# ScalarE's passes over the decay rows of a chunk, queued behind the rounding of the chunk in front

## The chip, the core and the metric

The kernel runs on one core of a Trainium2 chip. The metric is the time of one execution in microseconds (us) on the device. The engines are TensorE (PE in the profile, its weight loads PEld), VectorE (DVE), ScalarE (ACT), GpSimd (POOL) and SyncE (SP), which issues nearly all DMAs. Each engine runs its instructions in the order in which they stand in its own queue, and waits for other engines and for DMAs by semaphores.

## The reference, cut to what matters

One layer of a streaming encoder trunk on 2048 tokens of width 1024, in float32: RMSNorm, an input projection, two token mixers that read it (a short gated convolution and a Mamba-2 scan), an output projection, a second RMSNorm and a squared-ReLU MLP, and a last RMSNorm. The part that the change touches is the scan, here as the reference has it:

```
seg = a_cum[:, :, :, None] - a_cum[:, :, None, :]
decay = jnp.exp(jnp.where(causal[None, None, :, :, None, None], seg, -jnp.inf))
scores = jnp.einsum("bclgn,bcsgn->bclsg", c_c, b_c)
y_diag = jnp.einsum("bclsgr,bcsgrp->bclgrp", scores[..., None] * decay, x_c)
decay_end = jnp.exp(a_cum[:, :, -1:] - a_cum)
states = jnp.einsum("bclgn,bclgrp->bcgrpn", b_c, x_c * decay_end[..., None])
```

For each chunk of tokens and each head there is a matrix of decays, the exponential of a difference of running sums. It multiplies the scores, and the product multiplies the tokens' x (the diagonal part, y_diag). Beside that, x weighted by the decay up to the chunk's end is multiplied by B and added to a state that goes on to the next chunk.

## The kernel before, in words

The tokens lie in four blocks of 512 columns. Large products are float32 products made of three matmuls each: a rounded value (hi) and its remainder (lo) on both sides, hi by hi, hi by lo and lo by hi (`mm3`, L112 to L115, and L281 to L283 in `chain`). Rounding to hi is a ScalarE copy, the remainder a VectorE subtraction. The input projection and the MLP run seven half-size products in place of eight for each pair of tiles.

The program goes through these stages: the first half of the projection (to about 460 us), the second half with the first half of the scan beside it (to about 960 us), the output projection with the second half of the scan beside it (to about 1250 us), then the MLP up and down and the last norm. The scan is a generator: the loops of the stage take one piece of it after each product, so that its small instructions stand between the large matmuls. The order that each engine gets is then set by a scheduler, which takes the instructions by their place in the program, as they become ready in its own account of time; it may put an instruction of a later chunk ahead of one of an earlier chunk if that one isn't ready. `tc.issue_after(ins)` adds an edge to it: what is recorded inside stands behind `ins` on the engine of `ins`.

The scan has 32 steps (`CHUNKS`, L1212), numbered 0 to 31 here: for each block of 512 tokens, two groups of eight heads, four chunks of 128 tokens each. Steps 0 to 15 run beside the projection with one buffer of each kind, steps 16 to 31 beside the output projection with two (`bufs`, L1222). A step has these parts:

- `load` (L1238): DMAs of B and C (tile `bc`), of x (`xd`) and of the running sums of eight heads, broadcast to all partitions (`dec`, L1255, from `rd_d`).
- `front`, first piece (L1284 to L1296): TensorE transposes x and B (`ptx`, `ptb`) and multiplies B by C; ScalarE copies x to `xtok` (L1291) and rounds B (`btok`, L1293).
- `front`, second piece (L1299 to L1308): VectorE multiplies `xtok` by two weights (L1301). ScalarE rounds the product for the state (L1303, `xtok<-stmp`, the "rounding of weighted x"); VectorE makes its remainder (L1308). ScalarE goes over the decay rows: eight passes, one for each head (L1306, Relu with the head's bias), and one exponential over all (L1307).
- `front`, third piece: ScalarE scales x by D (L1311), VectorE multiplies the decays by the masked scores (L1312).
- `back` (L1315): TensorE multiplies B by the rounded x (`st`, L113 to L115), C by the state (`yo`, L1326) and the decays by x (`yd`, L1329). VectorE combines them (L1338 to L1345), ScalarE squares (L1348) and takes a root (L1356) for a norm, and a DMA stores the result.

The passes over the decay rows need only a DMA, while the rounding needs TensorE, ScalarE and VectorE in turn. With two buffers the rows of step n+1 are on the chip while step n is under way, and so the scheduler places passes of step n+1 ahead of the rounding of step n. Beside the scan, ScalarE also rounds the weights of the output projection (L100, `whi`) and the blocks of mixer output that it multiplies (L1458 scales `ry` after a DMA, L1459 rounds it).

Of the kernel before, what the change touches and what calls it, by code (L numbers as in the profile page):

```python
# [2 lines left out]

# [1 line left out]

# [8 lines left out]
AF = mybir.ActivationFunctionType  # L14
# [11 lines left out]
HG = 8  # L26
# [14 lines left out]
def trunk(ctx: ExitStack, tc: tile.TileContext, x, w_in, w_dt, w_out, w_up, w_down, cvec, hrow, out):  # L41
    nc = tc.nc
# [42 lines left out]
    def col(base, i):  # L85
        return cv[:, base + i : base + i + 1]
# [37 lines left out]
    def psum(tag, name, bufs=1):  # L124
        if tag in turns:
            tag = next(turns[tag])
        return ps.tile([P, 512], F32, tag=tag, name=name, bufs=bufs)

    class Rstd:


        def __init__(self, pool, tmp, n, w):
            self.pool, self.tmp, self.scale, self.w, self.n = pool, tmp, 1.0 / n, w, w // P
# [1078 lines left out]
    CHUNKS = [(b, g, c) for b in range(NB) for g in range(G) for c in range(NC)]  # L1212

    class Scan:
        def __init__(self, pool):
            self.state = []
            for g in range(G):
                s0 = pool.tile([P, 512], F32, name=f"state{g}")
                nc.vector.memset(s0, 0.0)
                self.state.append(s0)  # L1220
# [57 lines left out]
        def front(self, n):  # L1278

            b, g, c, h, ts, r0 = self.place(n)  # L1280
            t = self.got[n]
            bT, cT = t["bc"][:, 0], t["bc"][:, 1]
            byhead = lambda a: a.rearrange("p (h d) -> p h d", h=HG)
            pt = psum("tp", "ptx", 2)  # L1284
            for j in range(4):
                nc.tensor.transpose(pt[:, j * P : (j + 1) * P], t["xd"][:, j], ident)
            pb = psum("tp", "ptb", 2)
            nc.tensor.transpose(pb[:, 0:P], bT, ident)
            nc.tensor.matmul(pb[:, P : 2 * P], bT, cT, start=True, stop=True)
            xtok = self.tile([512], "xtok", 1)  # L1290
            nc.scalar.copy(xtok, pt)  # L1291
            hi, lo = t["btok"] = self.tile([P], "btok", 1).bitcast(F32R), bT.bitcast(F32R)
            nc.scalar.copy(hi, pb[:, 0:P])  # L1293
            nc.vector.tensor_tensor(out=lo, in0=pb[:, 0:P], in1=hi.bitcast(F32), op=ALU.subtract)
            sm = self.tile([L], "smask", 1)
            nc.vector.tensor_tensor(out=sm, in0=pb[:, P : 2 * P], in1=tri, op=ALU.mult)  # L1296
            yield

            for k, by in (("xde", "dend"), ("xdt", "dt")):  # L1299
                t[k] = self.tmp()  # L1300
                nc.vector.tensor_tensor(out=byhead(t[k]), in0=byhead(xtok), in1=t[by], op=ALU.mult)  # L1301
            hi, lo = t["parts"] = [a.bitcast(F32R) for a in (self.tile([512], "xtok", 1), self.tmp())]
            nc.scalar.copy(hi, t["xde"])  # L1303
            dec = t["dec"]
            for i in range(HG):
                nc.scalar.activation(dec[:, i], dec[:, i], AF.Relu, bias=t["a"][:, i : i + 1], scale=-1.0)  # L1306
            nc.scalar.activation(dec, dec, AF.Exp, scale=-1.0)  # L1307
            nc.vector.tensor_tensor(out=lo, in0=t["xde"], in1=hi.bitcast(F32), op=ALU.subtract)  # L1308
            yield
            for j in range(4):  # L1310
                nc.scalar.mul(t["xd"][:, j], t["xd"][:, j], col(C_D, 4 * g + j))  # L1311
            nc.vector.tensor_tensor(out=dec, in0=dec, in1=sm.unsqueeze(1).to_broadcast([P, HG, L]), op=ALU.mult)  # L1312
            yield
# [49 lines left out]
        def run(self, begin, end):  # L1363
# [10 lines left out]
            if self.bufs == 1:  # L1374
                for n in range(begin, end):
                    back = self.back(n)
                    front = self.front(n + 1) if n + 1 < end else iter(())
                    next(back)
                    yield
                    next(back)  # L1380
                    self.load(n + 1)
                    self.load_rows(n + 1)
                    yield
                    next(back)
                    yield
                    yield
                    next(front, None)
                    yield
                    next(back)
                    yield  # L1390
                    next(front, None)
                    yield
                    next(back)
                    self.load_gate(n + 1)
                    yield
                    next(front, None)
                    yield
                return
# [281 lines left out]
```

## Time and profile before

| | |
|---|---|
| median of 3 runs | 2637.45 us (2635.89 to 2637.7) |
| the profiled execution's own time | 2629.58 us |
| its span, first to last instruction | 2627.8 us |
| busy: PE, PEld, DVE, ACT | 99%, 81%, 73%, 55% of the span |
| mean granted TensorE clock | 0.998 |
| DMA, read from and written to HBM | 354.89 MB, 179.83 MB |

A group's line in the profile names the line of the kernel, the engine, the operation, the tiles (written <- read) and shapes, the count, the busy time with the mean duration, and the time that the engine sat idle just before, with what ended it. A line of the timeline begins with its start and its duration in us, and has such an idle time in brackets at its end. A matmul of 512 columns is shown for 0.39 us, but in an undisturbed row the next one starts 0.23 us later: they overlap, so a wait of TensorE is read from the starts. Matmuls in plain float32 show as two records each.

### The profile page before, as it was taken

How to read it: one execution, taken by the hardware profiler on the slowest of the kernel's cores; microseconds unless marked ns; L12 is line 12 of the kernel's file. 1: busy time of each engine (PE TensorE's matmuls, PEld its weight loads, DVE VectorE, ACT ScalarE, POOL GpSimd, SP SyncE). 2: the span in 40 equal slices, each digit the busy share in tenths (PEclk: the TensorE clock that was granted, in tenths of full speed). 3: DMA queues.
4: the chain of work that ended last, by engine and by line, in shares of the span. 5: the costliest groups of instructions: out<-in, count | busy, mean ns of one | idle time of the engine just before them, and what ended most of it. 6: DMA issues, size and time to landing. Idle time of an engine off the chain costs nothing.

```text
span 2627.8 us, 33775 instructions
## 1 busy us (share of the span) xinstructions
PE 2602.0 (99%) x12136; PEld 2140.6 (81%) x12136; DVE 1918.4 (73%) x2634; ACT 1455.3 (55%) x2211; POOL 55.7 (2%) x98
## 2 busy tenths in 40 slices
PE   9999999999999999999999999999999999999998
PEld 7888888788888888888888888888887788888887
DVE  7978867777778777878777765644448777888985
ACT  6654345776667676867336555655555444444443
POOL 0010000000000000000000000000000000000001
PEclk9999999999999999999999999999999999999999
DMA  3545745555555588877666786855558544665762
GB/s 147 203 171 192 273 144 194 190 167 172 176 167 164 165 281 255 267 225 223 201 201 235 271 311 229 285 205 206 186 200 288 154 152 151 208 213 170 247 208 77
DMA packets 252167, 536.96 MB, mean 204 GB/s; under 512 B 26208, under 2 KB 93024, under 8 KB 252000
## 3 DMA queue, kind: packets, MB, share of 16 engines
q1 hardware_dynamic: 251856, 534.29, 60.8%
q8 instruction: 95, 1.56, 0.2%
q14 instruction: 72, 0.59, 0.1%
q10 hardware_dynamic: 144, 0.52, 0.1%
HBM read 354.89 MB, written 179.83 MB: 203 GB/s over the span
## 4 chain that ended last, share of the span: by engine, by line
PE 65%; issue 24%; DMA 4%; ACT 3%; DVE 3%; SPq 0%; POOL 0%; POOLq 0%; DVEq 0%; ACTq 0%
PE px L281 10%; PE px L283 10%; PE px L282 10%; PE py L281 5%; PE py L282 5%; PE py L283 5%; PE pm L114 4%; PE pm L113 4%; PE pm L115 3%; PE pw L281 2%; PE pw L283 2%; PE pw L282 2%; DMA dec<-rd_d 1%; PE yd L1329 1%; PE yo L1326 1%
## 5 line engine op out<-in xcount | busy, mean ns | idle before, releaser
L281 PE MATMUL px<-uh,whi 128*128 128x512 f32 x1672 | 656.4, 393 | 9.6 <-DVE acc L1051 6.4
L282 PE MATMUL px<-ul,whi 128*128 128x512 f32 x1672 | 651.7, 390 | 0.0
L283 PE MATMUL px<-uh,wlo 128*128 128x512 f32 x1672 | 651.6, 390 | 0.0
L281 PEld LDWEIGHTS px<-uh,whi 128*128 128x128 f32 x1672 | 314.1, 188 | 83.7 <-DVE acc L1051 6.0
L101 DVE TENSOR_TENSOR wlo<-wraw,whi 128x1024 fp32r<-128x1024 f32 x214 | 222.6, 1040 | 202.6 <-ACT whi L100 202.5
L283 PEld LDWEIGHTS px<-uh,wlo 128*128 128x128 f32 x1672 | 314.3, 188 | 66.0 <-issue 0.2
L282 PEld LDWEIGHTS px<-ul,whi 128*128 128x128 f32 x1672 | 314.2, 188 | 63.7
L100 ACT CAST whi<-wraw 128x1024 fp32r<-128x1024 f32 x214 | 193.9, 906 | 309.3 <-PE px L282 219.2
L100 ACT CAST whi<-s 128x1024 fp32r<-128x1024 f32 x210 | 219.8, 1047 | 224.0 <-PE py L282 95.9
L281 PE MATMUL py<-uh,whi 128*128 128x512 f32 x836 | 327.1, 391 | 1.1 <-ACT eb L784 0.8
L282 PE MATMUL py<-ul,whi 128*128 128x512 f32 x836 | 325.8, 390 | 0.0
L283 PE MATMUL py<-uh,wlo 128*128 128x512 f32 x836 | 325.5, 390 | 0.0
L101 DVE TENSOR_TENSOR wlo<-s,whi 128x1024 fp32r<-128x1024 f32 x210 | 255.3, 1216 | 70.2 <-ACT whi L100 68.5
L113 PE MATMUL pm<-uh,whi 128*128 128x512 f32 (+1 forms) x648 | 250.9, 388 | 0.1
L114 PE MATMUL pm<-ul,whi 128*128 128x512 f32 (+1 forms) x648 | 248.2, 383 | 0.4 <-DVE ul L211 0.2
L115 PE MATMUL pm<-uh,wlo 128*128 128x512 f32 (+1 forms) x648 | 247.9, 383 | 0.0
L281 PEld LDWEIGHTS py<-uh,whi 128*128 128x128 f32 x836 | 157.1, 188 | 35.6 <-ACT eb L784 1.2
L283 PEld LDWEIGHTS py<-uh,wlo 128*128 128x128 f32 x836 | 156.9, 188 | 32.7
L282 PEld LDWEIGHTS py<-ul,whi 128*128 128x128 f32 x836 | 157.0, 188 | 32.3
L352 ACT CAST uh<-rh 128x1024 fp32r<-128x1024 f32 (+1 forms) x128 | 120.2, 943 | 85.3 <-PE py L283 67.2
L281 PE MATMUL pw<-uh,whi 128*128 128x512 f32 x418 | 163.3, 391 | 0.0
L283 PE MATMUL pw<-uh,wlo 128*128 128x512 f32 x418 | 162.7, 389 | 0.0
(242 smaller groups left out, 3788.4 us busy)
## 6 DMA issues: line engine op xcount, KB each, us to landing
hid_d<-e SPq DMA_DIRECT2D x96, 512.0 KB, 3.7
rh<-hid_d SPq DMA_DIRECT2D x96, 512.0 KB, 4.4
wraw<-w_in SPq DMA_DIRECT2D x68, 512.0 KB, 4.0
wraw<-w_down SPq DMA_DIRECT2D x104, 256.0 KB, 3.6
wraw<-w_up SPq DMA_DIRECT2D x48, 512.0 KB, 4.2
dec<-rd_d SPq DMA_DIRECT2D x32, 512.0 KB, 5.1
wraw<-w_out SPq DMA_DIRECT2D x32, 512.0 KB, 4.7
x_d<-xt SPq DMA_DIRECT2D x64, 256.0 KB, 3.8
```

The source lines that it names most:

```text
L100: nc.scalar.copy(hi, raw)
L101: eng.tensor_tensor(out=lo, in0=raw, in1=hi.bitcast(F32), op=ALU.subtract)
L113: nc.tensor.matmul(out, whi, hi, start=(k == 0), stop=False)
L114: nc.tensor.matmul(out, whi, lo, start=False, stop=False)
L115: nc.tensor.matmul(out, wlo, hi, start=False, stop=(k == nk - 1))
L281: nc.tensor.matmul(p, hi, h[0], start=not seeded and k == 0, stop=False, **kw)
L282: nc.tensor.matmul(p, hi, h[1], start=False, stop=False, **kw)
L283: nc.tensor.matmul(p, lo, h[0], start=False, stop=(k == len(g) - 1), **kw)
L352: nc.scalar.copy(p[i][0], t)
L1326: nc.tensor.matmul(yo[:, j * L : (j + 1) * L], state[:, j * P : (j + 1) * P], cT, start=True, stop=True)
L1329: nc.tensor.matmul(yd[(i % 2) * 64 : (i % 2) * 64 + 64, (i // 2) * L : (i // 2 + 1) * L], byhead(t["xdt"])[:, i, :], t["dec"][:, i % 2 * 4 ...
```

## The change

In `front`, the eight passes over the decay rows are recorded ahead of the rounding, and inside `tc.issue_after` of the rounding of the step before. No instruction is added, taken away or given another size.

```
     class Scan:
+        cast = None
+
...
             hi, lo = t["parts"] = [a.bitcast(F32R) for a in (self.tile([512], "xtok", 1), self.tmp())]
-            nc.scalar.copy(hi, t["xde"])
             dec = t["dec"]
-            for i in range(HG):
-                nc.scalar.activation(dec[:, i], dec[:, i], AF.Relu, bias=t["a"][:, i : i + 1], scale=-1.0)
+            with tc.issue_after(self.cast.ins) if self.cast else nullcontext():
+                for i in range(HG):
+                    nc.scalar.activation(dec[:, i], dec[:, i], AF.Relu, bias=t["a"][:, i : i + 1], scale=-1.0)
+            self.cast = nc.scalar.copy(hi, t["xde"])
             nc.scalar.activation(dec, dec, AF.Exp, scale=-1.0)
             nc.vector.tensor_tensor(out=lo, in0=t["xde"], in1=hi.bitcast(F32), op=ALU.subtract)
```

In the changed kernel the lines stand two or three further down: the passes are L1308, the rounding L1309, the exponential L1310, and the copy to `xtok` L1293, the copy for `btok` L1295, the scaling by D L1314, the square L1351, `ry` L1461 and L1462. In the following pieces of ScalarE's queue the numbers behind the tiles tell buffers apart: `dec_9565` belongs to step 24, `xtok_9651` to step 23, `dec_10669` to step 30, `xtok_10759` to step 29, `dec_9376` to step 23 and `xtok_9452` to step 22.

ScalarE around the rounding of step 23, before:

```order
L1306 ACTIVATE dec_9565<-dec_9565,dd_9558 128x128 x5
L1348 ACTIVATE stmp_9618<-y_9427 128x512
L1291 COPY xtok_9592<-ptx_9584 128x512
L1293 CAST btok_9594<-ptb_9589 128x128
L1311 ACTIVATE xd_9374<-xd_9374,cv_154 128x128 x4
L1306 ACTIVATE dec_9565<-dec_9565,dd_9558 128x128 x3
L1458 ACTIVATE ry_10310<-ry_10310,cv_154 128x512
L1303 CAST xtok_9651<-stmp_9647 128x512
```

The same place with the change:

```order
L1461 ACTIVATE ry_10310<-ry_10310,cv_154 128x512
L1351 ACTIVATE stmp_9618<-y_9427 128x512
L1314 ACTIVATE xd_9374<-xd_9374,cv_154 128x128
L1293 COPY xtok_9592<-ptx_9584 128x512
L1295 CAST btok_9594<-ptb_9589 128x128
L1314 ACTIVATE xd_9374<-xd_9374,cv_154 128x128 x3
L1309 CAST xtok_9651<-stmp_9647 128x512
L1308 ACTIVATE dec_9565<-dec_9565,dd_9558 128x128 x7
```

The eight passes of step 24 stood ahead of the copy to `xtok` and of the rounding of step 23; they now stand behind the rounding.

ScalarE around the rounding of step 29, before:

```order
L1306 ACTIVATE dec_10669<-dec_10669,dd_9558 128x128 x4
L1348 ACTIVATE stmp_10733<-y_10537 128x512
L1311 ACTIVATE xd_10480<-xd_10480,cv_154 128x128
L1291 COPY xtok_10707<-ptx_10699 128x512
L1528 ACTIVATE sq_10696<-xt_10577 128x512
L1293 CAST btok_10709<-ptb_10704 128x128
L1311 ACTIVATE xd_10480<-xd_10480,cv_154 128x128 x3
L1306 ACTIVATE dec_10669<-dec_10669,dd_9558 128x128 x4
L1459 CAST uh0_10900<-ry_10680 128x512
L1307 ACT_TABLE_LOAD
L1307 ACTIVATE dec_10669<-dec_10669 128x1024
L1303 CAST xtok_10759<-stmp_10755 128x512
```

The same place with the change:

```order
L1462 CAST uh0_10900<-ry_10680 128x512
L1351 ACTIVATE stmp_10733<-y_10537 128x512
L1293 COPY xtok_10707<-ptx_10699 128x512
L1295 CAST btok_10709<-ptb_10704 128x128
L1314 ACTIVATE xd_10480<-xd_10480,cv_154 128x128
L1531 ACTIVATE sq_10696<-xt_10577 128x512
L1314 ACTIVATE xd_10480<-xd_10480,cv_154 128x128 x3
L1309 CAST xtok_10759<-stmp_10755 128x512
L1308 ACTIVATE dec_10669<-dec_10669,dd_9558 128x128 x5
```

Here the eight passes, the table load and the exponential of step 30 stood ahead of the rounding of step 29, and now stand behind it.

In one place the rounding gets something new in front of it. ScalarE around the rounding of step 22, before:

```order
L1306 ACTIVATE dec_9376<-dec_9376,dd_8313 128x128 x5
L1303 CAST xtok_9452<-stmp_9448 128x512
L1306 ACTIVATE dec_9376<-dec_9376,dd_8313 128x128 x3
L1458 ACTIVATE ry_9487<-ry_9487,cv_154 128x512
L1307 ACT_TABLE_LOAD
```

And with the change:

```order
L1461 ACTIVATE ry_9487<-ry_9487,cv_154 128x512
L1309 CAST xtok_9452<-stmp_9448 128x512
L1308 ACTIVATE dec_9376<-dec_9376,dd_8313 128x128 x8
L1462 CAST uh1_9713<-ry_9487 128x512
L1310 ACT_TABLE_LOAD
```

The scaling of `ry_9487`, which waits for a DMA, stood behind the rounding of step 22 and now stands ahead of it. The same holds at step 28 with `ry_10676`.

Outside of ScalarE less moves. TensorE's order differs only about the small matmuls of steps 0, 16, 17 and 18, VectorE's in step 0 and from step 17 on. In the first half of the scan ScalarE's order differs in steps 0 and 1 alone; the rounding of step 0 stands behind eight of its own passes where it stood behind seven, and that of step 16, which opens the second half, behind eight where it stood behind six. Some DMAs change places with a neighbour in SyncE's queue.

More of the change, by code (lines that the diff above doesn't have):

```diff
@@ L1 @@
 import itertools
-from contextlib import ExitStack
+from contextlib import ExitStack, nullcontext
 import numpy as np
```

## The prediction

> **What bounds the kernel now.** I read the page first, for the share of each engine.
>
> ```profile
> span 2627.8 us, 33775 instructions
> PE 2602.0 (99%) x12136; PEld 2140.6 (81%) x12136; DVE 1918.4 (73%) x2634; ACT 1455.3 (55%) x2211; POOL 55.7 (2%) x98
> ```
>
> TensorE is busy nearly throughout; its idle time is 2627.8 - 2602.0 = 25.8 us. The change touches ScalarE, so it can give back only what TensorE loses to ScalarE, or take more of it. Where TensorE loses time in the second half of the scan is told by the waits of TensorE between 960 and 1252 us, and by the busy times in stretches of 50 us (columns: PE, PEld, DVE, ACT, POOL, granted clock, DMA share, GB/s).
>
> ```profile
> PE st L113 <- ACT xtok L1303: 1.3, 2, 0.9
> PE st L114 <- DVE stmp L1308: 1.1, 3, 0.6
> ```
>
> ```profile
> 1000.00:1050.00 50.00, 50.00 (x279) 41.66 (x278) 35.75 (x56) 28.18 (x57) 0.00 (x0) 1.00 0.86 272
> 1050.00:1100.00 50.00, 48.99 (x267) 40.31 (x266) 39.72 (x65) 44.63 (x89) 0.00 (x0) 1.00 0.89 278
> 1200.00:1250.00 50.00, 48.58 (x263) 39.77 (x264) 39.70 (x65) 33.02 (x65) 0.00 (x0) 1.00 0.68 206
> ```
>
> All of TensorE's waits there are of `st`, the product with the rounded x: for the rounding itself, and for its remainder, which VectorE makes of it. They lie in two of the stretches. Then ScalarE's own waits, between 960 and 1260 us, show why the rounding is late.
>
> ```profile
> ACT dec L1306 <- DMA dec<-rd_d: 23.7, 10, 5.1
> ACT ry L1458 <- DMA ry<-yn_d: 6.7, 4, 2.3
> ```
>
> The passes over the decay rows of the next step stand in the queue before their DMA has landed, and ScalarE stops for it; everything behind stops too. The timeline of ScalarE at step 23:
>
> ```profile
> 1090.08 1.57 ACT L1306 ACTIVATE dec<-dec,dd 128x128 f32<-128x128 f32 x5 [2.48 <-DMA dec<-rd_d]
> ...
> 1092.08 0.56 ACT L1291 COPY xtok<-ptx 128x512 f32<-128x512 f32 x1
> ...
> 1093.89 0.98 ACT L1306 ACTIVATE dec<-dec,dd 128x128 f32<-128x128 f32 x3
> ...
> 1095.38 0.61 ACT L1303 CAST xtok<-stmp 128x512 fp32r<-128x512 f32 x1
> ```
>
> TensorE at the same step, at step 29 and at step 30, and at step 28, where nothing is waited for:
>
> ```profile
> 1095.22 0.39 PE L115 MATMUL pm<-uh,wlo 128*128 128x512 f32 x1
> 1096.04 0.51 PE L113 MATMUL st<-xtok,btok 128*128 128x512 f32 x1 [0.43 <-ACT xtok L1303]
> 1097.12 0.50 PE L114 MATMUL st<-stmp,btok 128*128 128x512 f32 x1 [0.58 <-DVE stmp L1308]
> ...
> 1097.69 0.49 PE L1326 MATMUL yo<-bc,state 128*128 128x128 f32 x3
> ```
>
> ```profile
> 1207.32 0.39 PE L115 MATMUL pm<-uh,wlo 128*128 128x512 f32 x1
> ...
> 1209.91 1.05 PE L1326 MATMUL yo<-bc,state 128*128 128x128 f32 x8
> ```
>
> ```profile
> 1226.47 0.39 PE L115 MATMUL pm<-uh,wlo 128*128 128x512 f32 x1
> ...
> 1227.96 1.05 PE L1326 MATMUL yo<-bc,state 128*128 128x128 f32 x8
> ...
> 1229.97 0.50 PE L113 MATMUL pm<-uh,whi 128*128 128x512 f32 x1
> ```
>
> ```profile
> 1189.86 0.39 PE L115 MATMUL pm<-uh,wlo 128*128 128x512 f32 x1
> 1190.09 0.40 PE L113 MATMUL st<-xtok,btok 128*128 128x512 f32 x1
> ...
> 1190.79 1.05 PE L1326 MATMUL yo<-bc,state 128*128 128x128 f32 x8
> ```
>
> From the start of the last large matmul to the start of `yo`, the undisturbed step takes 1190.79 - 1189.86 = 0.93 us. Step 23 takes 2.47, step 29 takes 2.59, step 30 takes 1.49.
>
> **The change, part by part.** *The three waits.* They cost 1.54 + 1.66 + 0.56 = 3.76 us of TensorE. How much earlier does the rounding come? At step 23 the five passes and their wait go from in front of the copy to `xtok`: 2.48 + 1.57 us, and three more passes (about 0.9) from in front of the rounding. The one thing that takes their place there, the scaling of `ry`, stood ahead of the rounding before too. So both ends of the chain copy, product, rounding come some 4 us earlier, where 1.54 are needed. At step 29 the eight passes go (at 0.3 us from one to the next, 2.4 us), and with them a table load and an exponential:
>
> ```profile
> 1205.70 1.28 ACT L1307 ACT_TABLE_LOAD   x1
> ...
> 1207.96 0.60 ACT L1303 CAST xtok<-stmp 128x512 fp32r<-128x512 f32 x1
> ```
>
> From 1205.70 to 1207.96 that is 2.26 us, so 4.7 us with the passes, where 1.66 are needed. At step 30 eight passes go, 2.4 us, where 0.56 are needed. I take all 3.76 us. The lower end is what the profile calls idle in the two stretches, (50 - 48.99) + (50 - 48.58) = 2.43 us: a wait shorter than the overlap of two matmuls is not in it.
>
> [...]
>
> *Step 17.* Before, `st` and `yd` alternate:
>
> ```profile
> 984.36 1.05 PE L1326 MATMUL yo<-bc,state 128*128 128x128 f32 x8
> 985.16 0.47 PE L113 MATMUL st<-xtok,btok 128*128 128x512 f32 x1
> ...
> 987.61 0.50 PE L113 MATMUL pm<-uh,whi 128*128 128x512 f32 x1
> ```
>
> From `yo` to the next large matmul these are 3.25 us. With the change `yd` follows `yo`, and the `st` matmuls go between large ones. In the undisturbed order the same work costs 2.01 us from `yo` to the large matmul at step 30 and 3 x 0.23 for `st`, 2.70 together: a gain of 0.55 us for four changes fewer between small and large matmuls.
>
> *Step 16.* The rounding stands behind eight passes where it stood behind six, so 0.6 us later:
>
> ```profile
> 970.11 1.87 ACT L1306 ACTIVATE dec<-dec,dd 128x128 f32<-128x128 f32 x6
> 971.87 0.61 ACT L1303 CAST xtok<-stmp 128x512 fp32r<-128x512 f32 x1
> ```
>
> TensorE asks for it two large matmuls (0.46 us) later than before, so a loss of 0.1 us is left, between 0 and the 0.6. Two more changes between small and large matmuls there, and two fewer in step 18, cancel. Step 0 is alike: one pass more in front, two large matmuls more as cover, taken as nothing.
>
> *What goes behind the rounding.* The passes and the exponential of step n+1 come up to 5 us later in ScalarE's queue. Who needs them is VectorE's product with the masked scores of step n+1, a whole step later:
>
> ```profile
> 1097.30 1.06 ACT L1307 ACTIVATE dec<-dec 128x1024 f32<-128x1024 f32 x1
> ```
>
> ```profile
> 1112.08 1.22 DVE L1312 TENSOR_TENSOR dec<-dec,smask 128x1024 f32<-128x1024 f32 x1
> ```
>
> The exponential of step 24 ends at 1098.36, its reader starts at 1112.08: 13.7 us of cover, and nothing is charged. Should a step lose its cover, `yd` and TensorE would wait for the excess. Nor does the DMA wait come back: where the DMA of step 24 landed at 1090.08, the passes now start behind a rounding at about 1091.5. So most of the 23.7 us that ScalarE waits for `dec` goes, but ScalarE is no bound; of this only the rows above count. The weights' rounding (L100) stands about where it stood. SyncE issues the same DMAs, a few in swapped places, at nothing.
>
> The sum is -3.76 - 0.55 + 0.1 = -4.2 us. Against the profiled execution, 2629.58 becomes 2625.4. The three runs' median is 7.87 us above that execution, which no row here explains; taking the difference over, 2637.45 becomes **2633.2 us**, 0.16% less. About 0.2% (5.3 us) is what a measurement of this kernel can tell from no change, so this counts as the same.
>
> **The rivals.** *More than the forecast.* The timed runs are 7.87 us longer than the profiled one. If they wait longer for the DMA of the decay rows, more than three of the sixteen steps are pushed over their margin, and the change gives that back too; in the profiled execution the longest of the ten waits for `dec` is already 5.1 us. One more step like 29, 1.66 us, brings 2631.6, two 2629.9. Against it: nothing says that the extra time lies here. Chance 0.23.
>
> *Nothing is left.* The gain is swallowed where TensorE waits later on:
>
> ```profile
> L281 PE MATMUL px<-uh,whi 128*128 128x512 f32 x1672 | 656.4, 393 | 9.6 <-DVE acc L1051 6.4 <-ACT s L894 1.5 <-ACT s L746 0.7
> ```
>
> If the chains that end these 9.6 us (most behind 1250 us) ran by the clock of their DMAs and not by TensorE's progress, the stretch in front could shrink and the wait grow by it: 2637.5. Against it: those DMAs fetch what earlier products stored, and start when these are done. Chance 0.12.
>
> *Slower.* At steps 22 and 28 the rounding now stands behind the scaling of `ry`, and so behind a DMA. In the row of waits above the longest wait for it was 2.3 us. ScalarE and TensorE at step 22, before:
>
> ```profile
> 1075.10 0.73 ACT L1458 ACTIVATE ry<-ry,cv 128x512 f32<-128x512 f32 x1
> ```
>
> ```profile
> 1077.99 0.40 PE L113 MATMUL st<-xtok,btok 128*128 128x512 f32 x1
> ```
>
> Put behind the scaling as it stands, the rounding (0.61) would end by 1076.4, 1.6 us ahead of TensorE. So it decides from a `ry` that lands 1.6 us later than that scaling. With 6.6 us at both steps TensorE would wait 5 us twice, and run slower behind each wait:
>
> ```profile
> 2039.11 0.47 PE L281 MATMUL px<-uh,whi 128*128 128x512 f32 x1 [2.90 <-DVE acc L1051]
> ...
> 2040.56 0.63 PE L283 MATMUL px<-uh,wlo 128*128 128x512 f32 x1
> 2040.98 0.63 PE L281 MATMUL px<-uh,whi 128*128 128x512 f32 x1
> ```
>
> Behind a wait of 2.90 us some eight matmuls started 0.43 us apart and not 0.23, 1.6 us more. That is 10 + 3.2 - 4.2 = +9.0, or 2646.4 us. [...] Chance 0.06.
>
> That the change doesn't do what it says is not a rival: the rows of the order in the part on the change show the passes behind the rounding.
>
> **How the numbers follow.** The forecast has 0.59, more 0.23, nothing 0.12, slower 0.06. Faster by over 0.2% takes "more" and 0.03 of the forecast's edge, 0.26; within 0.2% are 0.56 + 0.12 = 0.68; slower 0.06. The range reaches from two more steps (2629.9) to nothing gained and the 0.6 us of step 16 lost (2638.1).
>
> **What would show it.** In the changed profile TensorE's waits for L1309 and its remainder are gone from 1000 to 1250 us, the stretches about steps 23, 29 and 30 have near 41.6 us of weight loads, ScalarE's wait for `dec` falls from 23.7 to under 3 us, and the span is about 2623.6. I am wrong if TensorE waits for `yd`'s decays or for a rounding behind `ry`, or if those waits vanish and the span stays.

## The result, and the profile after

The changed kernel took 2631.51 us in the median of 19 runs (2625.54 to 2635.45), the kernel before 2637.01 us in the 19 runs beside it (2632.69 to 2641.8). The ratio is 0.9979, with an interval of 0.9973 to 0.9986: 5.5 us less, between 3.7 and 7.1, or 0.21%. That is inside the predicted range, 1.7 us below the predicted time, and at the edge between "within 0.2%" and "faster".

The profiled execution doesn't show that gain. The page of the changed kernel:

```profile
span 2628.9 us, 33767 instructions
PE 2602.4 (99%) x12136; PEld 2140.5 (81%) x12136; DVE 1918.7 (73%) x2634; ACT 1455.0 (55%) x2211; POOL 56.1 (2%) x98
```

Its own time is 2631.37 us, near its median, and 1.8 us more than the profiled execution of before. That one, 2629.58 us, was shorter than each of the 19 timed runs of its kernel. So two questions stand: what the change did between these two traces, and what an ordinary execution of before loses that the profiled one did not.

TensorE's waits between 960 and 1252 us with the change, and ScalarE's for DMAs between 960 and 1260 us:

```profile
PE st L114 <- DVE stmp L1311: 1.1, 1, 1.1
```

```profile
ACT ry L1461 <- DMA ry<-yn_d: 9.5, 6, 4.5
ACT dec L1308 <- DMA dec<-rd_d: 0.7, 1, 0.7
```

The waits of steps 23, 29 and 30 are gone, and ScalarE's wait for `dec` is 0.7 us instead of 23.7. But the span is 2628.9 us and not the forecast 2623.6: "those waits vanish and the span stays" was one of the signs by which the prediction would call itself wrong. And one wait of `st` is new. The stretches of the changed kernel show where it lies, and a second loss that was not forecast (columns as in the prediction):

```profile
450.00:500.00 50.00, 47.26 (x228) 36.08 (x227) 35.23 (x60) 38.20 (x67) 0.00 (x0) 1.00 0.71 235
500.00:550.00 50.00, 48.58 (x251) 36.92 (x250) 38.34 (x77) 38.76 (x63) 1.18 (x4) 1.00 0.50 157
1050.00:1100.00 50.00, 50.00 (x270) 41.60 (x270) 40.18 (x68) 41.47 (x85) 0.00 (x0) 1.00 0.91 270
1100.00:1150.00 50.00, 48.81 (x267) 40.08 (x264) 35.74 (x58) 33.12 (x64) 0.00 (x0) 1.00 0.81 246
1200.00:1250.00 50.00, 50.00 (x269) 41.73 (x269) 40.99 (x67) 34.85 (x68) 0.00 (x0) 1.00 0.71 212
```

And before, in the first two of them:

```profile
450.00:500.00 50.00, 47.96 (x232) 36.99 (x230) 37.92 (x65) 40.27 (x71) 0.00 (x0) 1.00 0.71 229
500.00:550.00 50.00, 49.98 (x259) 38.52 (x258) 37.14 (x73) 37.62 (x61) 1.18 (x4) 1.00 0.56 176
```

The stretches about steps 23, 29 and 30 are full, with 41.60 and 41.73 us of weight loads. The one about step 24 has lost 1.5 us of them, and those about steps 0 and 1 have lost 0.9 and 1.6 us.

Both traces hold 12136 matmul records, in the same order but for a few places. So the start of the k-th in one less its start in the other is a running account of what was lost and won. After less before, by the time in before:

| at us | 450 | 490 | 506 | 550 | 960 | 980 | 1094 | 1100 | 1120 | 1206 | 1212 | 1232 | 1255 | 2600 |
|---|---|---|---|---|---|---|---|---|---|---|---|---|---|---|
| lag, us | +0.45 | +1.32 | +2.78 | +3.14 | +2.99 | +3.12 | +2.56 | +1.06 | +2.79 | +2.79 | +1.13 | +0.59 | +0.60 | +0.87 |

From 450 to 550 us, about steps 0 and 1, 2.69 us were lost, 1.46 of them between 490 and 506 us, at step 1. Step 16 cost 0.13. Step 17 gave 0.53, step 23 1.50, step 29 1.66 and step 30 0.54. Step 24 took 1.73. What lies before 450 us is the spread of identical code, and between 450 and 490 us the spread is as large as the loss there: over that stretch the seven other traces that keep the order of before at steps 0 and 1 differ from the first profile by -0.7 to +1.5 us.

Why step 24 waits: ScalarE with the change, from the rounding of step 23 to that of step 24.

```profile
1096.47 0.62 ACT L1309 CAST xtok<-stmp 128x512 fp32r<-128x512 f32 x1 [1.14 <-DVE stmp L1303]
1097.00 2.15 ACT L1308 ACTIVATE dec<-dec,dd 128x128 f32<-128x128 f32 x7
...
1101.66 0.72 ACT L1461 ACTIVATE ry<-ry,cv 128x512 f32<-128x512 f32 x1 [1.27 <-DMA ry<-yn_d]
...
1108.38 1.34 ACT L1461 ACTIVATE ry<-ry,cv 128x512 f32<-128x512 f32 x2 [1.80 <-DMA ry<-yn_d]
...
1112.41 0.57 ACT L1293 COPY xtok<-ptx 128x512 f32<-128x512 f32 x1
...
1115.16 0.62 ACT L1309 CAST xtok<-stmp 128x512 fp32r<-128x512 f32 x1 [1.42 <-DVE stmp L1303]
```

The passes behind the rounding wait for nothing now. The scaling of `ry` behind them waits for its DMA, twice, 3.07 us in all, and behind that stand the root of the norm and the copy to `xtok` of step 24. In both traces the root starts 2.7 us after the last of these fetches of `ry` has landed, so the landing sets the chain. It comes at 1103.64 us before and at 1108.30 with the change, 3.6 us later by TensorE's progress. The fetch was issued later and took longer to land, 6.5 us and not 5.0. In SyncE's queue a fetch of weights (`wraw`) stood behind it, and with the change stands ahead of it:

```profile
1098.68 0.43 SPq L1445 DMA_DIRECT2D ry<-yn_d  x1
1100.58 0.34 SPq L95 DMA_DIRECT2D wraw<-w_out  x1
```

```profile
1101.38 0.34 SPq L95 DMA_DIRECT2D wraw<-w_out  x1
1101.77 0.48 SPq L1448 DMA_DIRECT2D ry<-yn_d  x1
```

The rounding of step 24 ends at 1115.78. TensorE finds it just in time, and waits for the remainder:

```profile
1115.38 0.39 PE L115 MATMUL pm<-uh,wlo 128*128 128x512 f32 x1
1115.83 0.51 PE L113 MATMUL st<-xtok,btok 128*128 128x512 f32 x1
1117.46 0.50 PE L114 MATMUL st<-stmp,btok 128*128 128x512 f32 x1 [1.12 <-DVE stmp L1311]
```

Why step 1 loses: ScalarE at step 1 with the change, and, below it, in the kernel with the edit in the second half alone (the first experiment), where steps 0 and 1 stand as before.

```profile
492.67 0.99 ACT L1308 ACTIVATE dec<-dec,dd 128x128 f32<-128x128 f32 x3 [1.76 <-DMA dec<-rd_d]
...
494.97 0.26 ACT L659 ACTIVATE dts<-dts 128x64 f32<-128x64 f32 x1
```

```profile
489.91 0.69 ACT L1313 ACTIVATE dec<-dec,dd 128x128 f32<-128x128 f32 x2
...
491.92 0.26 ACT L659 ACTIVATE dts<-dts 128x64 f32<-128x64 f32 x1
```

Three passes of step 1 instead of two stand ahead of the exponential for dt, and they wait 1.76 us for the rows of step 1. The third pass is worth only some 0.3 us, and the two needed the same rows. What differs is the landing: the rows came 6.4 us after their issue here and 4.7 us after it there, where the passes then found them. In SyncE's queue one of the two fetches of B and C (`bc`) stands ahead of the two of `eb` here and behind them there. VectorE's chain for dt hangs on that exponential, and TensorE on the chain:

```profile
503.14 0.41 PE L677 MATMUL pc<-dts,tri 128*128 128x64 f32 x2 [1.40 <-DVE dts L671]
```

### The profile page after: what moved, and what is told of

The parts are those of the page before. It is cut to its first block, busy times and chain, and to the rows that moved or that the text cites. A ratio compares the mean times of both kernels' runs of the same rounds, so it can differ in the third digit from the quotient of the medians.

```text
span 2628.9 us, 33767 instructions
## 1 busy us (share of the span) xinstructions
PE 2602.4 (99%) x12136; PEld 2140.5 (81%) x12136; DVE 1918.7 (73%) x2634; ACT 1455.0 (55%) x2211; POOL 56.1 (2%) x98
## 4 chain that ended last, share of the span: by engine, by line
PE 67%; issue 24%; DMA 3%; DVE 3%; ACT 2%; SPq 0%; POOL 0%; POOLq 0%; DVEq 0%; ACTq 0%
PE px L281 10%; PE px L282 9%; PE px L283 9%; PE py L281 5%; PE py L283 5%; PE py L282 5%; PE pm L113 4%; PE pm L114 4%; PE pm L115 4%; PE pw L281 2%; PE pw L283 2%; PE pw L282 2%; PE yd L1332 1%; PE yo L1329 1%; DMA ry<-yn_d 1%
```

## The experiments

The short diffs are against the changed kernel unless said otherwise. Ratios are to the kernel before, run beside each; a ratio is estimated from the single runs, and need not be the quotient of the two medians.

### The edit in the second half only, and in the first half only

The other kernel has 1 in place of the 2.

```
+            if self.bufs == 2:
                 with tc.issue_after(self.cast.ins) if self.cast else nullcontext():
...
             self.cast = nc.scalar.copy(hi, t["xde"])
+            if self.bufs != 2:
+                for i in range(HG):
+                    nc.scalar.activation(dec[:, i], dec[:, i], AF.Relu, bias=t["a"][:, i : i + 1], scale=-1.0)
```

> The edit is made only in the second half of the scan (steps 16 to 31); steps 0 and 1 keep the order of before. Theory (the traces: steps 0 and 1 cost TensorE about 2.3 us in the changed kernel, by the new waits for dts at 501 us and for the rounding at 480 us): the loss goes and the gain stays, -5.5 - 2.3 = about -7.8 us against before, ratio 0.9970, and TensorE has no wait for VectorE's dts L671 of 1.4 us. Rival (what was lost at steps 0 and 1 belongs to the one profiled execution): no faster than the changed kernel, -5.5 us, ratio 0.9979.

Measured: 2629.42 us against 2635.49, ratio 0.9984 (0.9974 to 0.9993). ScalarE does not wait for `dec` at step 1 (the rows above), and TensorE has no wait for `dts` there. The interval, -6.9 to -1.8 us, holds the rival's -5.5 and not the theory's -7.8 us; the two medians differ by 6.1. So by the times the theory missed, though the wait that it named is gone.

> The edit is made only in the first half (steps 0 to 15), where it moves instructions only at steps 0 and 1; steps 16 to 31 keep the order of before. Theory: slower than before by the loss at steps 0 and 1, about +2.3 us, ratio 1.0009, and the waits of st at steps 23, 29 and 30 are as before. Rival 1 (the loss was one execution's): no difference, 0 us. Rival 2 (the gain in the medians is made in the first half, where only the profiled pair shows a loss): -3 us or more.

Measured: 2636.81 against 2635.49 us, ratio 1.0005 (0.9996 to 1.0013), so a loss of up to 3.4 us or nothing; a gain of 3 us in the first half is excluded. In its second half this kernel has the order of before, and there its trace is not that of the first profile of before. At step 23:

```profile
1097.37 0.49 PE L113 MATMUL st<-xtok,btok 128*128 128x512 f32 x1 [1.00 <-ACT xtok L1310]
1098.44 0.50 PE L114 MATMUL st<-stmp,btok 128*128 128x512 f32 x1 [0.59 <-DVE stmp L1315]
...
1099.01 1.75 PE L1333 MATMUL yo<-bc,state 128*128 128x128 f32 x8
```

```profile
1096.00:1100.00 4.00, 2.42 (x11) 1.66 (x10) 3.59 (x6) 3.97 (x6) 0.00 (x0) 0.90 0.94 312
1100.00:1104.00 4.00, 4.00 (x26) 3.23 (x26) 3.35 (x5) 3.19 (x5) 0.00 (x0) 0.68 0.94 276
```

The wait for the rounding is 1.00 us where it was 0.43, and behind it the granted clock falls to 0.68 over 4 us: eight `yo` matmuls take 1.75 us where step 28 took 1.05. On the count of matmuls step 23 costs 3.7 us here against 1.54 in the first profile.

### The order of ScalarE alone, and the order of recording alone

In the first kernel the rounding is recorded first, as before, and only the edge is kept; in the second the passes are recorded first, without the `with` line. The diff is the first one's.

```
+            last, self.cast = self.cast, nc.scalar.copy(hi, t["xde"])
-            with tc.issue_after(self.cast.ins) if self.cast else nullcontext():
+            with tc.issue_after(last.ins) if last else nullcontext():
                 for i in range(HG):
                     nc.scalar.activation(dec[:, i], dec[:, i], AF.Relu, bias=t["a"][:, i : i + 1], scale=-1.0)
-            self.cast = nc.scalar.copy(hi, t["xde"])
```

> The rounding is recorded first, as before, and only the order on ScalarE is forced: the passes of a step behind the rounding of the step in front. TensorE's order is that of before everywhere, steps 0, 1 and 16 to 18 included. Theory (the gain comes from the rounding no longer standing behind the passes and their DMA): nearly all of the second half's gain without the loss at steps 0 and 1, but without step 17's 0.5 us: -7.3 us, ratio 0.9972; the waits of st at steps 23, 29 and 30 are gone. Rival (the gain comes from TensorE's own order, st between large matmuls): nothing, 0 to -1 us.

Measured: 2629.97 against 2635.49 us, ratio 0.9979 (0.9971 to 0.9988), -5.5 us (-7.6 to -3.2): the theory's -7.3 is in the interval, the rival's nothing far outside.

> The passes are recorded ahead of the rounding, without the forced order: TensorE's order is that of the changed kernel everywhere, while on ScalarE the passes of the next step still stand ahead of the rounding after step 17. Theory: the waits at steps 23, 29 and 30 stay (3.8 us in the profile), step 17 gains 0.5 and steps 0 and 1 lose 2.3 us: +1.8 us, ratio 1.0007. Rival (the gain comes from TensorE's own order): -4 us or more, ratio 0.9985 or less.

Measured: 2635.95 against 2635.49 us, ratio 1.0007 (0.9997 to 1.0017), as the theory had it; the rival's 0.9985 is excluded. TensorE's wait for the rounding between 960 and 1252 us:

```profile
PE st L113 <- ACT xtok L1308: 4.3, 3, 2.4
```

These waits are at steps 20, 23 and 29. So the gain is made by the order forced on ScalarE. The order of recording adds its 0.5 us at step 17 and the loss at step 1.

### One step at a time

The base is the kernel with the order of ScalarE alone; the edge is kept for one step, and in the counterpart `if n in (30, 31)`.

```
-            with tc.issue_after(last.ins) if last else nullcontext():
+            with tc.issue_after(last.ins) if n == 24 else nullcontext():
```

> Of the change only one place is kept: the eight passes of step 24 behind the rounding of step 23. TensorE's and SyncE's orders are those of before everywhere. Theory (step 23 is where an ordinary execution of before loses most: in the profiles that keep its order there, TensorE's wait for the rounding was 0.4, 1.8 and 2.4 us, and behind the two longer ones the granted clock fell to 0.68 to 0.85 over 4 us; on the count of matmuls the step cost 1.5, 3.6 and 4.8 us): -1.5 to -4.8 us, some -3.3 us, ratio 0.9987, and no granted clock under 1 near 1100 us. Rival (each wait counts as in the first profiled execution, and the rest of the medians' gain lies elsewhere): -1.5 us, ratio 0.9994.

Measured: 2633.44 against 2635.02 us, ratio 0.9990 (0.9981 to 0.9999), -2.6 us (-5.0 to -0.3); the medians differ by 1.6. That holds the theory's -3.3 and the rival's -1.5. (Of the three waits that the expectation names for step 23, the 1.8 us was at step 29 of its trace; at step 23 that trace had the 1.00 us shown above.) No wait is left at step 23. But at step 29, where this kernel has the order of before, its trace shows the dearest place of all:

```profile
1207.76 0.39 PE L115 MATMUL pm<-uh,wlo 128*128 128x512 f32 x1
1211.66 0.79 PE L113 MATMUL st<-xtok,btok 128*128 128x512 f32 x1 [3.51 <-ACT xtok L1306]
```

```profile
1212.00:1216.00 4.00, 4.00 (x19) 3.21 (x20) 2.80 (x5) 3.52 (x6) 0.00 (x0) 0.50 0.71 237
```

A wait of 3.51 us, then half the clock: 6.9 us against an undisturbed step, where the first profile lost 1.66.

> The counterpart: only the passes of steps 30 and 31 are put behind the rounding of steps 29 and 30; step 23 stays as in before. Theory: the 1.66 and 0.54 us of these two steps, and nothing of step 23: -2.2 us, ratio 0.9992; the profile shows TensorE's wait for the rounding at step 23 with a granted clock under 1 behind it if the wait is over about 1 us. Rival (what the medians gained over the profiled pair lies here): -4 us or more.

Measured: 2631.33 against 2635.02 us, ratio 0.9983 (0.9973 to 0.9994), -4.5 us (-7.1 to -1.6); the medians differ by 3.7. The theory's -2.2 and the rival's -4 are both in the interval. That step 29 can cost more than the theory's 1.66 us, and by the same mechanism, is told by the rows of step 29 just shown. TensorE's two longest waits in this kernel between 960 and 1252 us:

```profile
PE st L113 <- ACT xtok L1306: 2.1, 2, 1.9
PE pss L1357 <- DVE facc L1532: 2.0, 1, 2.0
```

The first is mostly step 23's, as forecast. The rest of it, 0.20 us, is at step 26, where the first profile has no wait. There ScalarE stood still for the rows of step 27 ahead of the rounding of step 26:

```profile
1148.87 1.58 ACT L1309 ACTIVATE dec<-dec,dd 128x128 f32<-128x128 f32 x5 [6.49 <-DMA dec<-rd_d]
```

On the count of matmuls 0.9 us are lost there. The kernel with the edge for step 23 alone lost 1.0 us at step 26, and the one with the order of recording alone 1.2 us at step 20; no trace in which the passes of every step of the second half stand behind loses anything at these two steps. The second wait in the list is new: `pss`, the sum for a norm behind step 29, comes late. By the ratios the two parts add to -7.1 us, by the medians to -5.3; the whole gave -5.5.

### Another profile of before

The kernel before, with no edit.

> The kernel before, unchanged, for another profile of it. Theory: an ordinary execution loses more at step 23 than the first profiled one: a wait of st over 1 us there, a granted clock under 1 behind it in the 4 us after, and 2 us or more between the two profiles on the count of matmuls from 1094 to 1100 us. Rival: waits of 0.4 to 0.6 us as in the first one, and the difference to the first profile lies outside 960 to 1260 us.

Measured: 2633.36 us in the profiled execution. The theory holds at step 23:

```profile
1096.57 0.39 PE L115 MATMUL pm<-uh,wlo 128*128 128x512 f32 x1
1098.81 0.51 PE L113 MATMUL st<-xtok,btok 128*128 128x512 f32 x1 [1.85 <-ACT xtok L1303]
1099.89 0.50 PE L114 MATMUL st<-stmp,btok 128*128 128x512 f32 x1 [0.58 <-DVE stmp L1308]
```

```profile
1100.00:1104.00 4.00, 4.00 (x27) 3.36 (x28) 2.95 (x5) 3.99 (x7) 0.00 (x0) 0.63 0.90 283
```

ScalarE here, at the passes of step 24:

```profile
1092.85 1.57 ACT L1306 ACTIVATE dec<-dec,dd 128x128 f32<-128x128 f32 x5 [1.94 <-DMA dec<-rd_d]
```

The rows of step 24 landed at 1092.85, where the first profile had 1090.08. TensorE was 1.35 us later too at that place (1096.57 against 1095.22), so they came 1.4 us later as TensorE sees it, and `st` waited 1.4 us more (1.85 against 0.43). The rest of the 2.86 us between the two profiles from 1094 to 1100 us, 1.4 us, goes with the clock: 0.63 over 4 us, where the first profile has 1.00, is 0.37 x 4 = 1.5 us. So the amount of the change's gain at step 23 is set by when a DMA lands, and the five traces with the order of before at step 23 show it together: by TensorE's progress the rows landed 0, 0.6, 1.4, 1.4 and 2.0 us later than in the first profile, and `st` waited 0.43, 1.00, 1.85, 1.87 and 2.41 us for the rounding.

### Fetching ry earlier

The base is the kernel with the order of ScalarE alone.

```
-            put(1, 0, 1, 34, (38, 40, 42, 44))
+            put(1, 0, 1, 30, (38, 40, 42, 44))
```

> The kernel with the forced order alone (TensorE's order of before), and in it the fetches of the first block of ry from the stored scan output are recorded four hooks earlier, so that they can land earlier. Theory (the new wait of 1.1 us at step 24 comes from ScalarE standing at the scaling of ry for its DMA, ahead of step 24's root and copy): no wait of st at step 24, ScalarE's wait for ry under 4 us in all (8 to 10 before), and the time as with the forced order alone or up to 1.6 us better, -5.5 to -7.1 us against before. Rival (the fetches wait for a free buffer, and land no earlier): ScalarE's wait for ry stays at 8 us, time -5.5 us.

Measured: 2630.9 against 2635.02 us, ratio 0.9982 (0.9971 to 0.9992). ScalarE still waits for it:

```profile
ACT ry L1461 <- DMA ry<-yn_d: 9.4, 5, 3.3
```

The wait for `ry` stays, `st` still waits 0.7 us at step 24, and nothing is won, as the rival said. But the edit did not move the fetches that step 24 stands behind. It moves the four of one block, which are scaled between 1067 and 1089 us, and three of them landed earlier. The two waits ahead of step 24 are for the second and the fourth fetch of the next block, recorded by the line below, and these were issued no earlier (at 1095.36 and 1100.32 us, where the kernel without this edit had 1094.48 and 1098.81). What fetching these earlier would give was not tested, and nothing here shows the rival's reason, a buffer that isn't free.

### The changed kernel beside the edit in the second half only, again

Both are as above, with no further edit.

> The changed kernel, unchanged, to set it beside the kernel with the edit in the second half only on one chip, and for another profile. Theory (at step 1 ScalarE stands still for the DMA of dec with three passes in front of the exponential for dt, where two stood before; in the three profiles with this order TensorE waited 1.4, 1.4 and 0.3 us for dts, in the seven with the other order 0 to 0.2): again a wait of ScalarE for dec between 488 and 494 us of 0.6 us or more, and 1 to 2.3 us lost on the count of matmuls between 450 and 550 us; about -5.5 us against before, ratio 0.9979. Rival (the loss there is no property of the order): no such wait, under 0.5 us lost there.

Measured: 2629.47 against 2635.62 us, ratio 0.9978 (0.9970 to 0.9987). At step 1:

```profile
492.42 0.99 ACT L1308 ACTIVATE dec<-dec,dd 128x128 f32<-128x128 f32 x3 [0.84 <-DMA dec<-rd_d]
```

The wait is there again, and TensorE waits 0.5 us for `dts`. On the count of matmuls 2.2 us are lost from 450 to 550 us, within the theory's 1 to 2.3, but only 0.5 of them between 490 and 506 us, where that wait lies; the rest came earlier, before the passes of step 1.

> The kernel with the edit in the second half only (steps 0 and 1 as before), again, beside the changed kernel. Theory: faster than the changed kernel by 1 to 2.3 us (mean of the profiles: 1.6), -7 us against before, ratio 0.9973; no wait of ScalarE for dec at step 1. Rival: the same as the changed kernel within 0.5 us.

Measured: 2628.86 against 2635.62 us, ratio 0.9973 (0.9964 to 0.9982). No wait for `dec` at step 1; 0.6 us faster than the changed kernel beside it, so the times don't decide between theory and rival. The traces show that the loss belongs to the order, and that it is smaller than the theory had it. Loss between 490 and 506 us against the first profile, in the four traces with the new order of steps 0 and 1:

| | order of recording alone | changed | changed, again | first half only |
|---|---|---|---|---|
| rows of step 1 landed after their issue, us | 6.8 | 6.4 | 5.6 | 5.4 |
| ScalarE waited for them, us | 2.0 | 1.8 | 0.8 | 0.6 |
| lost, us | 1.7 | 1.5 | 0.5 | 0.3 |

In the eight traces with the order of before at steps 0 and 1 the rows landed 4.0 to 4.8 us after their issue, ScalarE did not wait, and none of the seven lost over 0.1 us against the first. The edit in the second half only has no lead in time that is measured.

Its trace also has the dearest form of the other new wait, that of `pss`. ScalarE and TensorE behind step 29:

```profile
1212.73 0.73 ACT L1465 ACTIVATE ry<-ry,cv 128x512 f32<-128x512 f32 x1 [2.08 <-DMA ry<-yn_d]
...
1214.75 1.06 ACT L1314 ACTIVATE dec<-dec 128x1024 f32<-128x1024 f32 x1
...
1218.08 0.58 ACT L1535 ACTIVATE sq<-xt 128x512 f32<-128x512 f32 x1
```

```profile
1219.43 0.49 PE L1361 MATMUL pss<-ssq,ones_r 128*128 128x128 f32 x2 [3.02 <-DVE facc L1536]
```

The scaling of `ry` waits for its DMA, and the exponential that used to stand ahead of it stands behind. Behind both stands `sq<-xt`, the squares of a block of the output, which VectorE adds to `facc`. In this half of the scan the kernel gives `pss` and `sq` the same buffer (both are `psum("mw", ...)`), so `pss` waits until VectorE has read `sq`, 3 us; the sums that it reads itself, `ssq`, were written at 1203.94 us.

## Why the prediction was right, and where it was not

**The three waits.** Forecast 3.76 us; between the two traces 1.50 + 1.66 + 0.54 = 3.70. The steps were chosen rightly and sized rightly for that execution, and in the two stretches the weight loads tell more than the idle time: against the 41.66 us of the undisturbed stretch they lack 1.35 and 1.89 us, or 3.24 x 50 / 41.66 = 3.9 us of time, where the idle time is 2.43 us. The rounding of step 23 came only 1.5 us earlier by TensorE's progress, and not some 4 (up to 3.4 in the other traces with this order); it was enough.

**Steps 17 and 16.** Forecast -0.55 and +0.1, measured -0.53 and +0.13.

**Step 0, "alike, taken as nothing", and SyncE's swapped DMAs, "at nothing".** These steps failed. The prediction looked at the rounding of step 0 alone and not at step 1, where passes that need a DMA stand ahead of the exponential for dt. With the new order that DMA lands later, and step 1 cost 1.5 us in the first trace, 1.0 us in the mean of four, against at most 0.1 in the others.

**What goes behind the rounding, "nothing is charged".** Rightly for its own reader: TensorE nowhere waits for the exponential's product, and VectorE waits for the exponential once in the second half, for 0.2 to 1.1 us, where the first profile has 1.1. Wrongly for the DMA that stands next in ScalarE's queue. Behind the passes ScalarE comes to the scaling of `ry`, with the root and the next copy queued behind it, and the last fetch of `ry` ahead of step 24 lands later than it did. In the six traces with the passes of every step of the second half behind, what step 24 lost follows that landing (against the first profile, by TensorE's progress):

| us | order of ScalarE alone | `ry` earlier | second half, again | second half | changed | changed, again |
|---|---|---|---|---|---|---|
| landed later by | 1.8 | 2.9 | 3.1 | 3.4 | 3.6 | 4.8 |
| lost at step 24 | 0 | 1.0 | 1.1 | 1.5 | 1.7 | 2.9 |

From issue to landing this fetch took 6.5 to 8.8 us in these six and 4.4 to 5.0 us in the five with the order of before at step 23. In all six the fetch of weights stands ahead of it, in all five behind it. That the swapped places make the two transfers, this one and the rows of step 1, land later was not tested: no run restores SyncE's order alone. At 1217 us `pss` waited 0 to 3.0 us. ScalarE's wait for `ry` rose from 6.7 to 9.5 us.

**The rival "slower"** named the right transfer and the wrong place. At steps 22 and 28, where the rounding stands right behind the scaling, nothing waited. The price was paid at the next step, by the copy and the root.

**"More than the forecast"** is what happened: 2631.6 us was its time, 2631.51 was measured. Against it stood that nothing said where the extra 7.87 us of the timed runs lay. Part of them may lie at steps 23 and 29. Loss of a step against an undisturbed pass, on the count of matmuls, in all traces that keep the order of before there:

| us | first profile | other traces with that order |
|---|---|---|
| step 23 | 1.54 | 3.7, 4.1, 4.4, 4.9 |
| step 29 | 1.66 | 2.2, 2.5, 2.6, 6.9 |

So the profile on which the sum was made was the mildest of five at both steps. The rival thought of further steps being pushed over their margin. That happened in three of the six traces that keep the order of before at steps 20 and 26, for about 1 us each; in the main it was the same steps, waiting longer, and the clock behind them (0.63, 0.68 and 0.70 over 4 us at step 23 in three of these traces, 0.50 at step 29 in one).

**The account.** By the means of these traces the change gives 3.7 at step 23, 3.2 at step 29, 0.5 at step 17, 0.3 at step 30 and 0.5 at steps 20 and 26. It takes 1.4 at step 24, 1.4 about step 30 and 1.0 at step 1: 4.4 us net. The timed runs say 5.5 (3.7 to 7.1). Four to seven traces of places that vary by several us are few, so the sizes are rough. That the forecast of 4.2 us came so near is luck in part: the gains were twice as large as its sum had them, and nearly half of them went again in losses that it had put at nothing.

## What to carry to other kernels

An instruction that waited for a DMA, in ScalarE's queue ahead of a short chain that TensorE needed, cost here as much as the DMA was late and more (rows that landed 0 to 2.0 us later, waits of `st` of 0.43 to 2.41 us, 1.54 to 4.9 us lost at step 23), and that varied from run to run: take the size of such a wait from several profiles, not one. Moving it behind the chain does not end the matter; read what comes to the head of the queue next, and whether that waits for a DMA too. Follow a changed order through every step where it differs, in the queue that issues the DMAs as well, before calling one nothing. And before an experiment on a wait, find the very instruction that ends it, or the edit moves another.

## What was not expected of the hardware

Behind the wait of 2.90 us that the prediction had seen the granted clock is 0.57 from 2040 to 2044 us in the first profile of before. It falls behind shorter waits too: behind 1.85 + 0.58 us of idle time at one step, to 0.63 over 4 us (the second profile of before), and behind 1.00 + 0.59 us, to 0.68 (the edit in the first half only). It does not fall behind each wait of that size. In the second trace of the changed kernel, at step 24, it stays at 1.00:

```profile
1117.52 0.50 PE L113 MATMUL st<-xtok,btok 128*128 128x512 f32 x1 [1.21 <-ACT xtok L1309]
1119.15 0.50 PE L114 MATMUL st<-stmp,btok 128*128 128x512 f32 x1 [1.13 <-DVE stmp L1311]
```

```profile
1116.00:1120.00 4.00, 1.66 (x8) 0.95 (x7) 4.00 (x6) 3.15 (x8) 0.00 (x0) 1.00 0.78 237
1120.00:1124.00 4.00, 4.00 (x33) 3.30 (x33) 3.96 (x7) 3.95 (x6) 0.00 (x0) 1.00 0.69 201
```

The length of the wait alone does not decide: 1.00 + 0.59 us of idle time have an effect in one execution, and 1.21 + 1.13 us none in another. What else decides was not tested.

The mean granted clock of whole runs shows how often it falls. It was 0.998 or more in 25 of 84 timed runs of before, in 4 of 12 each with one of the two places mended, in 26 of 31 of the changed kernel, and in 29 of 45 of the three others with both mended; 0.001 of the span is 2.6 us.
